# One decoder layer on one core: 1 KB instead of 16 for software DMA descriptors, three more 4 KB slots, 49 expert tiles fetched ahead

## The chip, the cores and the metric

The kernel runs on one core of a Trainium2 chip. The metric is the device time of one launch in microseconds (us); three runs of the kernel before gave 512.88, 513.37 and 514.83 us, and their median, 513.37 us, is what the changed kernel is held against. The engines are named PE (matmul), PEld (its weight load), DVE, ACT, POOL and SP; in this kernel every load and store is issued by SP.

## The reference, cut to what matters

The layer takes x of shape 256 x 1024 (float32). Four token mixers run side by side, are gated, summed and projected, and the result is normalised. The second half is a mixture of experts, and the tiles that the change fetches sooner belong to it:

```
lg, le = x @ wr_g, x @ wr_e            # router: group, then two experts of its eight
h  = silu(x @ w_gate[e]) * (x @ w_up[e]) * gate[e]
y += h @ w_down[e]                     # for each of 32 experts
x  = layer_norm(alpha * x + y)
```

`w_gate` and `w_up` are 1024 x 256 for each expert, `w_down` 256 x 1024: 3 MB for each expert, 96 MB for all 32, each read once.

## The kernel before, in words

**Slots.** Most working tiles of 4 KB on each of the 128 partitions (512 KB in all) come from a pool `rp` of `NW` = 35 slots: weights as they arrive (`w`), the halves that a weight is split into (`hi`, `lo`), activations and masks. `slot` takes one. A slot is given to a new tile only when the readers and writers of the tile that held it are done; whatever writes the new tile first (a DMA, ACT, DVE or POOL) waits for that. A second pool, `rb`, with `NR` = 13 slots, is opened when the token mixers have ended (`gen_X`), in the SBUF that they leave.

**Order.** The first half is a set of generators, one letter each, and the string `ORDER` says which of them takes its next step. The program's order on every engine is the order in which the steps are written down. `S` splits projection weights and loads the next ones (line 246), `P` multiplies, `A` to `D` are the mixers, `U` and `O` the output projection, `Q`, `R`, `Y`, `Z` and `E` the router, the normalisation (`nrm`, line 1417, which reads `xtok`) and the gather of the first group of experts. `L` is one step of `gen_L`, which calls `fetch`.

**Expert tiles.** The experts run in eight groups (`NQUAD`) of four. For a group come eight tiles of `mwg` (gate), eight of `mwu` (up) and eight of `mwd` (down), 512 KB each: 192 tiles in a fixed list, `stream`; the `mwd` tiles of the last two groups stand at its end. `fetch` takes the next tile of the list, gives it a slot, from `rb` or `rp` by its number (`RB <= n % (NR + NF) < RB + NR`, with `NF` = 33, so 46 slots in turn), and issues its DMA on SP (line 1235). `gen_L` fetches the first `NL` = 46 within `ORDER`; from then on each tile is fetched in `wload`, where its group begins to use tiles and none is left in the list of fetched ones. The last eight tiles are loaded in halves (line 1242).

**A group** is: gate and up products (line 1527, PE, four experts side by side), the transposes of the scatter matrix (1477), the gather for the next group (1429), silu and product (1547 to 1549), a transpose (1552), the down product (1496) and the scatter into the accumulated result (1514; 1642 for the last group). Behind the last group come the statistics (1649, 1661), the scaling (1610, 1614, POOL's 1669) and the stores (1615, 1677).

The DMAs are numbered over eight semaphores, DMAHW0 to DMAHW7 in turn, and each DMA's issue waits for the landing of the one eight before it; so eight are under way at most.

Of the kernel before, what the change touches and what calls it, by code (L numbers as in the profile page):

```python
# [113 lines left out]
def _layout(inp):  # L114
# [81 lines left out]
MID = 8  # L196
NEAR = 6

NW = 35
NR = 13  # L200
NF = 33
N2 = 19
N1 = 10
NL = 46
RB = 0
LATE = 2
WARM = 5
# [7 lines left out]
    "ADDSAAADDAAABAAAABADDDDBDDDBBDDBBPDBBSDBSBBBBBBDDPDDBBBPCBCBPCSBBCBASPCLCMMCCCCCDMNCMCMCPCCSCCNCPSCP"  # L215
    "PSCPMMNPSPSMPCNMMMCCCDMNPPMSMPSMPSNPMCXLLMLLLLLLLPSPSPSPMPSPPSLPNNMLLMLLLSPMSLMLPSPLPSMPSPMNNPMLPSPS"
    "MMMPSMPSMNNMMMLMMPLMPSPSUMMPMMPMUUSUMUPMMUMPMMMPOUOLMLLLLMLULLUOULLLULMOUULULLMOUUOUUOQOQLQQQQQQQQLQ"
    "QYYLQQUQQQQORLOLLLRLRQRRLRQRRQRRRRQRRRZQZQERRRRRRRLRREQEEQRRE"
)


def body(ctx, tc, I, out):
# [6 lines left out]
    cp = ctx.enter_context(tc.tile_pool(name="cp", bufs=1))  # L229
    rp = ctx.enter_context(tc.tile_pool(name="rp", bufs=NW))  # L230

# [7 lines left out]
    def slot(name, shape, pool=None, dt=F32):  # L239

        t = (pool or rp).tile([P, 1024], dt, tag="w", name=name)
        return view(t, int(np.prod(shape[1:])), shape)
# [986 lines left out]
    def fetch():  # L1229
        n = len(fetched)  # L1230
        src, (e, k), shape = stream[n]
        t = slot("w", shape, MP["rb"] if RB <= n % (NR + NF) < RB + NR else rp)
        fetched.append(t)
        if n < len(stream) - 8:
            SY.dma_start(t, I[src][e][k])
            return

        tails.append((t, I[src][e][k]))
        if n == len(stream) - 1:
            for hs in (slice(0, 512), slice(512, 1024)):  # L1240
                for t, a in tails:
                    SY.dma_start(t[:, hs], a[:, hs])

    def gen_L():
        yield "X"
        for i in range(NL):
            fetch()
            if i + 1 < NL:
                yield 0
# [498 lines left out]
```

## Time and profile before

| | |
|---|---|
| median of three runs | 513.37 us (512.88 to 514.83) |
| the profiled execution | 511.94 us, of which the span of its instructions 510.2 us |
| PE busy | 467.2 us, 92% of the span |
| PEld busy | 357.0 us, 70% |
| DVE / ACT / POOL busy | 241.7 / 195.8 / 47.0 us |
| bytes moved | 146.82 MB, 288 GB/s over the span |
| granted TensorE clock, mean | 0.981 |

The span holds two programs in a row: up to 300 us the mixers, the projection and the router, from 300 us on the eight groups of experts. Shares over the whole span are means of the two. In windows of 20 us and of the end the DMA engines are less than half busy between 60 and 200 us, and from 308 us until the loads end they are busy all the time.

### The profile page before, as it was taken

The page shows a single profiled execution, that of the slowest core. Times are in us where ns is not written, and L with a number is a line of the kernel's source. Part 1 is how long each engine was busy: PE and PEld are TensorE (multiplying, and loading weights), DVE is VectorE, ACT ScalarE, POOL GpSimd, SP SyncE. Part 2 cuts the span into 40 slices and gives each one's busy share as a digit, 9 for nine tenths or more (in the row PEclk, how much of TensorE's full clock was granted, in tenths as well). Part 3 has the DMA queues.
Part 4 walks back from the last instruction along what each step waited for, and adds up shares of the span by engine and source line. Part 5 has one row for each costly group of instructions (what it writes and reads, how often), then busy time and mean ns, then how long its engine had stood idle before and what let it go on. Part 6 is the DMA issues. An engine that isn't in the chain of part 4 may idle for free. (4 is left out here: it accounts for less than half of the span.)

```text
span 510.2 us, 10633 instructions
## 1 busy us (share of the span) xinstructions
PE 467.2 (92%) x4396; PEld 357.0 (70%) x4396; DVE 241.7 (47%) x479; ACT 195.8 (38%) x357; POOL 47.0 (9%) x55
## 2 busy tenths in 40 slices
PE   8999999999999999999999899998898989777891
PEld 6888887998778999999998676554453635343420
DVE  4786659987868558544764643021111211111015
ACT  5967555366494465434353342020201201001311
POOL 2003022300000012123150000000000000000002
PEclk9999999999999999999999989999999999989896
DMA  8999432212332452999879869999999999999962
GB/s 283 350 371 383 141 110 84 89 39 84 123 127 84 145 187 90 408 410 409 336 288 413 287 242 406 407 409 408 409 408 408 409 409 409 408 410 408 401 239 84
DMA packets 44410, 146.82 MB, mean 288 GB/s; under 512 B 4996, under 2 KB 7624, under 8 KB 44360
## 3 DMA queue, kind: packets, MB, share of 16 engines
q1 hardware_dynamic: 44360, 146.12, 75.0%
q8 instruction: 35, 0.57, 0.4%
q14 instruction: 15, 0.12, 0.1%
HBM read 143.48 MB, written 2.62 MB: 286 GB/s over the span
## 5 line engine op out<-in xcount | busy, mean ns | idle before, releaser
L374 PE MATMUL ps<-xl,hi 128*128 128x256 f32 x416 | 122.3, 294 | 1.9 <-DVE vS L385 1.1
L375 PE MATMUL ps<-xh,lo 128*128 128x256 f32 x416 | 118.0, 284 | 0.4 <-DVE lo L360 0.3
L376 PE MATMUL ps<-xh,hi 128*128 128x256 f32 x416 | 117.6, 283 | 0.0
L360 DVE TENSOR_TENSOR lo<-w,hi 128x1024 fp32r<-128x1024 f32 (+1 forms) x75 | 89.1, 1206 | 53.1 <-ACT hi L359 45.5
L374 PEld LDWEIGHTS ps<-xl,hi 128*128 128x128 f32 x416 | 79.7, 192 | 5.6 <-issue 1.9
L375 PEld LDWEIGHTS ps<-xh,lo 128*128 128x128 f32 x416 | 79.7, 192 | 2.6 <-issue 1.4
L359 ACT CAST hi<-w 128x1024 fp32r<-128x1024 f32 (+1 forms) x75 | 74.2, 1014 | 16.9 <-PE ps L375 5.1
L376 PEld LDWEIGHTS ps<-xh,hi 128*128 128x128 f32 x416 | 79.7, 192 | 0.0
L1527 PE MATMUL ps<-w,xg 128*32 128x256 f32 x1024 | 69.0, 393 | 7.8 <-DMA w<-mwu 7.0
L1527 PEld LDWEIGHTS ps<-w,xg 128*32 128x32 f32 x1024 | 34.0, 112 | 39.7 <-DMA w<-mwu 12.2
L1429 PE MATMUL ps<-Sel,nrm 128*128 128x128 f32 x256 | 33.6, 286 | 1.3 <-DVE smr L1395 0.7
L1429 PEld LDWEIGHTS ps<-Sel,nrm 128*128 128x128 f32 x256 | 31.3, 200 | 4.8 <-issue 4.1
L1514 PE MATMUL ps<-small,SGT 128*128 128x512 f32 x48 | 23.7, 616 | 9.1 <-DVE small L1508 5.1
L1508 DVE COPY small<-ps 128x512 f32<-128x512 f32 x6 | 4.2, 692 | 53.2 <-PE ps L1514 53.2
L1479 ACT COPY SGT<-ps 128x256 f32<-128x256 f32 x8 | 3.0, 373 | 65.8 <-PE ps L1477 65.8
L1496 PE MATMUL ps<-w,small 128*32 128x512 f32 x192 | 24.7, 599 | 3.7 <-ACT xg L1436 3.0
L1514 PEld LDWEIGHTS ps<-small,SGT 128*128 128x128 f32 x48 | 8.2, 189 | 24.9 <-DVE small L1508 10.1
L1669 POOL TENSOR_TENSOR res<-res,ln 128x512 f32<-128x512 f32 x1 | 1.7, 1730 | 239.2 <-ACT res L1668 239.2
L1422 DVE TENSOR_TENSOR Sel<-rank,csts 128x128 f32<-128x128 f32 x16 | 4.0, 288 | 32.7 <-PE ps L1477 32.7
L374 PE MATMUL ps<-parts,hi 128*128 128x256 f32 x64 | 18.8, 293 | 0.0
L1496 PEld LDWEIGHTS ps<-w,small 128*32 128x32 f32 x192 | 5.4, 109 | 18.3 <-ACT xg L1436 7.5
L375 PE MATMUL ps<-parts,lo 128*128 128x256 f32 x64 | 18.1, 283 | 0.0
(417 smaller groups left out, 703.2 us busy)
## 6 DMA issues: line engine op xcount, KB each, us to landing
w<-mwg SPq DMA_DIRECT2D x64, 512.0 KB, 10.2
w<-mwu SPq DMA_DIRECT2D x64, 512.0 KB, 10.2
w<-mwd SPq DMA_DIRECT2D x56, 512.0 KB, 10.2
w<-win SPq DMA_DIRECT2D x54, 512.0 KB, 5.4
w<-wbr SPq DMA_DIRECT2D x8, 512.0 KB, 4.1
w<-wout SPq DMA_DIRECT2D x8, 512.0 KB, 7.9
w<-mwd SPq DMA_DIRECT2D x16, 256.0 KB, 5.3
scr<-fsb SPq DMA_DIRECT2D x1, 1536.0 KB, 7.0
```

Source lines behind the costliest of these rows:

```text
L359: A.copy(hi, src)
L360: V.tensor_tensor(lo, src, hi.bitcast(F32), op=OP.subtract)
L374: T.matmul(dst, lhsT=ls[0], rhs=rs[1], start=start, stop=False)
L375: T.matmul(dst, lhsT=ls[1], rhs=rs[0], start=False, stop=False)
L376: T.matmul(dst, lhsT=ls[0], rhs=rs[0], start=False, stop=stop)
L1422: V.tensor_tensor(t, rank[q][:, 4 * g:4 * g + 4, None].broadcast_to([P, 4, 32]), C("iota")[:, None, :].broadcast_to([P, 4, 32]), op=OP.is_ ...
L1429: T.matmul(pg[:, k4], lhsT=nrm[q][:, 128 * k:128 * k + 128], rhs=f2(SelR[g, q]), start=q == 0 and k4 == 0, stop=True, skip_group_check=True)
L1479: A.copy(SGT, pg)
L1496: T.matmul(pd[h][32 * e4:32 * e4 + 32], lhsT=outs[g][0][:, k, 32 * e4:32 * e4 + 32], rhs=wds[g][k][e4][:, 512 * h:512 * h + 512], start=k ...
L1508: V.tensor_copy(dn[h], pd[h])
L1514: T.matmul(yacc[q, h], lhsT=outs[g][1][:, q], rhs=dn[h], start=False, stop=False, skip_group_check=True)
L1527: T.matmul(pgu[32 * e4:32 * e4 + 32, i], lhsT=xg[:, k, 32 * e4:32 * e4 + 32], rhs=ws[k // 4][e4][:, k % 4, :], start=k == 0, stop=k == KT ...
```

## The change

[...] 

```
-NW = 35
+NW = 38
 NR = 13
-NF = 33
+NF = 36
-NL = 46
+NL = 49
@@ the last row of ORDER
-    "QYYLQQUQQQQORLOLLLRLRQRRLRQRRQRRRRQRRRZQZQERRRRRRRLRREQEEQRRE"
+    "QYYLQQUQQQQORLOLLLRLRQRRLRQRRQRRRRQRRRZQZQERRRRRRRLRREQEEQRRELLL"
@@ def kernel
-    nc = _bacc.Bacc("TRN2", target_bir_lowering=False, num_devices=1)
+    nc = _bacc.Bacc("TRN2", target_bir_lowering=False, num_devices=1, dynamic_dma_scratch_size=1024)
```

No engine gets an instruction more or less, and none stands in another place in its engine's order. What differs is which slot a tile takes, and so what the first writer of a tile waits for. On SP, around the end of `ORDER`, the fetches stand as follows; the number behind `w_` counts the program's tiles, and a name in brackets is a semaphore: DMAHW0 to 7 of the DMA eight before, PE, Activation, DVE and Pool of the readers and writers of the tile that held the slot. Before:

```order
L1235 DMA w_3609<-mwd 128x1024 [waits DMAHW2_49,PE_49]
L1235 DMA w_3675<-mwd 128x1024 [waits DMAHW3_49,Activation_49]
L1235 DMA w_4012<-mwd 128x1024 [waits DMAHW4_49,PE_49]
L1235 DMA w_4014<-mwd 128x1024 [waits DMAHW5_49,PE_49]
L1235 DMA w_4054<-mwg 128x1024 [waits DMAHW6_49,PE_49]
L1235 DMA w_4056<-mwg 128x1024 [waits DMAHW7_49,PE_49]
L1235 DMA w_4058<-mwg 128x1024 [waits DMAHW0_49,PE_49]
```

And now:

```order
L1235 DMA w_3609<-mwd 128x1024 [waits DMAHW2_49,PE_49]
L1235 DMA w_3675<-mwd 128x1024 [waits DMAHW3_49,PE_49]
L1235 DMA w_3721<-mwd 128x1024 [waits DMAHW4_49]
L1235 DMA w_3723<-mwd 128x1024 [waits DVE_49,PE_49,DMAHW5_49,Activation_49,Pool_49]
L1235 DMA w_3725<-mwg 128x1024 [waits DMAHW6_49,Activation_49]
L1235 DMA w_4056<-mwg 128x1024 [waits DMAHW7_49,PE_49]
L1235 DMA w_4058<-mwg 128x1024 [waits DMAHW0_49,PE_49]
```

`w_3675` is the 46th fetch in both. Before, the 47th, 48th and 49th (`w_4012`, `w_4014`, `w_4054`) are written down in groups 1 and 2 of the experts and take the slots of the first, second and third fetched tile, which PE reads at line 1527 of group 0. Now (`w_3721`, `w_3723`, `w_3725`) they take slots of `rp` in which a tile of the router or the normalisation lay, and the 50th, `w_4056`, is the first to wait for PE's reading of the first fetched tile.

On POOL, at 44 us in the span, the clearing of `qx` (a tile of mixer C) takes another slot. Before:

```order
L667 TENSOR_TENSOR Cm<-LB,cst 128x256 [waits DVE_49]
L1027 MEMSET qx 128x1024 [waits Pool_49]
L686 TENSOR_TENSOR Cm<-LB,cst 128x256
L686 TENSOR_TENSOR Cm<-LB,cst 128x256 [waits PE_49,Activation_49]
L686 TENSOR_TENSOR Cm<-LB,cst 128x256 [waits PE_49,Pool_49]
```

And now:

```order
L667 TENSOR_TENSOR Cm<-LB,cst 128x256 [waits DVE_49]
L1027 MEMSET qx 128x1024 [waits DMAHW4_49,DVE_49]
L686 TENSOR_TENSOR Cm<-LB,cst 128x256
L686 TENSOR_TENSOR Cm<-LB,cst 128x256 [waits PE_49]
L686 TENSOR_TENSOR Cm<-LB,cst 128x256 [waits PE_49,Pool_49]
```

The slot is now one in which a weight lay that DVE reads at line 360 to make its `lo`; `Cm` (mixer D's triangular blocks) stand behind it on POOL.

## Rows read from the trace of the kernel before

**Rows 1.** Windows: stretch, length, PE, PEld, DVE, ACT, POOL busy, PEclk, DMA share, GB/s.
```profile
0.00:284.00 284.00, 278.13 (x2624) 253.30 (x2624) 191.64 (x324) 156.67 (x265) 43.97 (x53) 1.00 0.62 227
...
284.00:287.00 3.00, 2.76 (x17) 2.32 (x16) 1.35 (x7) 2.06 (x4) 0.00 (x0) 1.00 0.35 85
287.00:299.00 12.00, 10.05 (x65) 8.82 (x64) 6.56 (x29) 4.80 (x11) 0.00 (x0) 0.86 0.94 342
299.00:302.00 3.00, 3.00 (x54) 1.94 (x56) 2.14 (x12) 2.17 (x8) 0.00 (x0) 1.00 0.04 14
302.00:305.00 3.00, 3.00 (x54) 1.58 (x50) 1.25 (x6) 0.37 (x1) 0.00 (x0) 1.00 0.72 205
...
308.00:494.00 186.00, 163.06 (x1541) 86.03 (x1540) 30.01 (x87) 27.43 (x64) 0.00 (x0) 0.98 1.02 404
494.00:495.00 1.00, 1.00 (x3) 0.19 (x1) 0.65 (x1) 0.00 (x0) 0.00 (x0) 1.00 0.02 6
```

**Rows 2.** SP's waits, 312 to 500 us: total us, times, longest.
```profile
SPq L1235 <- DMA w<-mwu: 41.9, 47, 1.3
...
SPq L1235 <- PE ps L1527: 7.5, 10, 4.8
```

**Rows 3.** DMA: queue with packets, MB, share; issues with count, size, us to landing.
```profile
q1 hardware_dynamic: 44360, 146.12, 75.0%
...
w<-mwu SPq DMA_DIRECT2D x64, 512.0 KB, 10.2
```

**Rows 4.** PE's waits, 437 to 458 us (the group of experts before the last).
```profile
PE ps L1527 <- DMA w<-mwu: 3.7, 5, 1.1
...
PE ps L1527 <- DMA w<-mwg: 0.5, 1, 0.5
```

**Rows 5.** PE's waits, 458 to 500 us (the last group and the end).
```profile
PE ps L1527 <- DMA w<-mwu: 3.3, 5, 0.7
...
PE ps L1527 <- DMA w<-mwg: 0.4, 1, 0.4
```

**Rows 6.** Timeline of PE, 405 to 512 us; in brackets its wait and for what.
```profile
416.25 3.66 PE L1527 MATMUL ps<-w,xg 128*32 128x256 f32 x64
...
453.05 3.47 PE L1527 MATMUL ps<-w,xg 128*32 128x256 f32 x26 [0.66 <-DMA w<-mwu]
...
463.27 1.91 PE L1527 MATMUL ps<-w,xg 128*32 128x256 f32 x26 [0.40 <-DMA w<-mwg]
...
473.58 3.52 PE L1527 MATMUL ps<-w,xg 128*32 128x256 f32 x26 [0.66 <-DMA w<-mwu]
...
495.10 1.06 PE L1496 MATMUL ps<-w,hh 128*32 128x512 f32 x8
```

**Rows 7.** Windows at the granted clock's two low stretches, and in the end.
```profile
453.30:456.60 3.30, 3.30 (x27) 1.38 (x19) 0.00 (x0) 0.04 (x1) 0.00 (x0) 0.50 1.03 411
473.80:477.10 3.30, 3.29 (x26) 1.22 (x18) 0.00 (x0) 0.00 (x0) 0.00 (x0) 0.50 1.03 410
478.60:497.00 18.40, 17.62 (x111) 7.89 (x111) 2.09 (x3) 6.05 (x10) 0.00 (x0) 1.00 0.80 295
```

**Rows 8.** SP's waits, 255 to 312 us.
```profile
SPq L1235 <- PE ps L1527: 7.9, 2, 7.0
...
SPq L1235 <- ACT nrm L1417: 4.4, 1, 4.4
```

**Rows 9.** Timelines of ACT and PE near 300 us: start, length, what.
```profile
292.94 1.24 ACT L1417 ACTIVATE nrm<-xtok,nmr,mv 128x1024 f32<-128x1024 f32 x1 [1.34 <-DVE rank L1389]
...
299.53 3.66 PE L1527 MATMUL ps<-w,xg 128*32 128x256 f32 x64
```

**Rows 10.** Timelines of POOL and DVE near 44 us.
```profile
44.50 0.95 POOL L1027 MEMSET qx<- 128x1024 f32 x1
45.41 1.43 POOL L686 TENSOR_TENSOR Cm<-LB,cst 128x256 f32<-128x256 f32 x2
...
48.13 2.36 DVE L360 TENSOR_TENSOR lo<-w,hi 128x1024 fp32r<-128x1024 f32 x2 [4.00 <-ACT hi L359]
```

**Rows 11.** Tile Cm: its reader on PE (ns min/median/max, first to last start).
```profile
L635 PE MATMUL ps<-XY,Cm x160: 218/218/267, 62.2 to 109.4; 64*64 64x64 f32 x160
```

## The prediction

> **What bounds the kernel now.** I read windows first, because a share over the whole span mixes two programs. Up to 284 us PE is busy 278.13 of 284 us while the DMA engines are at 0.62 [rows 1]: PE is the bound there, and no fetch that comes sooner helps it. From 308 to 494 us the DMA share is 1.02 at 404 GB/s [rows 1]; in that stretch SP's own waits are for the DMA eight places before (41.9 us in 47 waits for the `mwu` tiles alone), and its waits for a slot, 7.5 us on PE's line 1527, are at most 4.8 us long [rows 2]. A tile lands 10.2 us after its issue with eight under way [rows 3], so a stall of 4.8 us on SP still leaves the engines tiles to move. From 308 us on the loads are thus one unbroken stream, and the last packets of it go at 494 us: the share falls to 0.02 in the next microsecond [rows 1].
>
> Does the end hang on that stream? PE's waits say where. PE lives on the stock of tiles fetched ahead; in the last two groups the stock is gone. It waits for tiles 3.7 + 0.5 = 4.2 us in the group before the last [rows 4] and 3.3 + 0.4 = 3.7 us in the last [rows 5], 7.9 us in all. The last `mwu` tile starts PE's final 26 products at 473.58, behind a wait of 0.66 us for it [rows 6]; what follows to the end of the span at 510.2 is PE's work at 17.62 of 18.40 us and then DVE's. And PE's last eight down products stand at 495.10 [rows 6], 1.1 us behind the last packets. So the end follows the stream, with 1.1 us of play at most.
>
> The third thing is when the stream starts. Between 299 and 302 us the DMA engines stand at 0.04 [rows 1]: SP waited 7.0 us in one piece for PE's line 1527 [rows 8], that is, for group 0 to free the slot of the first fetched tile, and its products begin at 299.53 [rows 9].
>
> **The change part by part.** Before, the fetches 47 to 49 are the ones that stand in this hole. In the order now, the 47th waits for nothing but the DMA before it, the 49th for Activation, and the 48th for all four engines, none of them at work in the experts yet. What ACT ends last among the tiles of `rp` is `nrm`, which reads `xtok`: 292.94 + 1.24 = 294.18 us [rows 9]. That is the release on which the 46th fetch stood before, for 4.4 us [rows 8]; now it is the 49th's. So all three are issued by about 294.5 us, some 7 us before PE frees the first expert tile.
>
> Is there room for them? Idle time of the DMA engines: 0.65 of 3 us from 284, 0.06 of 12 us from 287, 0.96 of 3 us from 299 [rows 1], or 2.0 + 0.7 + 2.9 = 5.6 us. A tile costs 10.2 / 8 = 1.28 us of the engines, three 3.8 us. They fit, and none of them delays the 50th, which now takes the place of the 47th behind the same PE instructions, with the same slow first microseconds (0.72 from 302 to 305 us [rows 1]). From there every tile lands when the one three places before it did: **3.8 us sooner**, to the last packets at 490.2. A slot's release behaves alike: each later fetch waits for the tile 49 before instead of 46, and lies three places further on.
>
> What PE makes of it: the final `mwu` tile comes at 469.8 instead of 473.58. Without any wait PE would stand there 7.9 us sooner, at 465.7; so it still waits for that tile and takes the 3.8 us in full, with 7.9 - 3.8 = 4.1 us of waits left. They vanish first where they come first: in the group before the last 4.2 - 3.8 = 0.4 us should be left, and all 3.7 in the last. From the last `mwu` tile on nothing is changed, and all of it moves by 3.8 us.
>
> [...]
>
> The granted clock is the term with two ends. [...] With 0.4 us of waits left in the group before the last I expect its low stretch to go; that brings PE 1.6 us nearer to tiles that have not landed, and turns into waiting in the last group (3.7 + 1.6 = 5.3 us). If the second one goes as well, PE could gain 1.6 us more behind the last `mwu` tile, but no more than the 1.1 us before it meets the last packets. If one falls into the 18.40 us that now run at 1.00 [rows 7], it costs 1.6 us. I take zero, as the pattern of tiles in the last group stays, and keep -1.1 and +1.6.
>
> Cost at nothing, with the cover named. Slots in the first 284 us: loads and ACT's and DVE's splits get theirs sooner or when they did; PE's 278.13 us hide it. POOL is the exception: the clearing of `qx`, done from 44.50, now waits for DVE's line 360, whose pair runs from 48.13 to 50.49 [rows 10], so up to 6.0 us; two `Cm` of 1.43 us stand behind it on POOL. They would end at about 52.9, and PE reads its first `Cm` at 62.2 [rows 11]: 9 us of cover. Without it the 6 us would go into mixer D's chain. The smaller descriptor space: the loads and stores go through the hardware queue, 44360 packets [rows 3], so nothing here writes descriptors by software. New addresses for tiles: the 64 gate products of a group take 3.66 us in group 0 [rows 9] and 3.66 in group 5 [rows 6], from other slots, so I take nothing on either side.
>
> Sum: the profiled execution took 511.94 us, 510.2 in the span and 1.7 around it. It becomes 506.4 + 1.7 = 508.1. The three timed runs lie 0.9 to 2.9 us above it, the median by 1.4; I carry that over: **509.5 us**.
>
> **Rivals.** (a) The three are not early. If a slot stayed held to group 0, as that of the 47th was (7.0 us [rows 8]), the stream starts as before: 513.4. The order speaks against it, the 47th's only wait being a DMA; for it, that the 48th waits for all four engines, and SP is in order, so one late release there holds everything behind it. (b) A low stretch of the clock moves into the end: 509.5 + 1.6 = 511.1. Rows 7 show that it falls after bursts with waits between, and the last group will have more of these.
>
> (c) Slower: the clock stays low through the end. PE, sooner at the last group, waits longer; where the low grant then lasts from 469.8 over the PE work of 17.62 us [rows 7], that takes up to 17.62 x 1.6 / 1.91 = 14.8 us more, 524 us. Half of it gives 517. It decides from 3.8 us of loss, or three low stretches in the end instead of none. Against it: both low stretches here ended while PE was in dense work, and 478.60 to 497 ran at 1.00. [...] (d) PE, not the stream, leads the end: no waits, 509.5 - 1.1 = 508.4 at best, being held by the last packets.
>
> **How the numbers follow.** The forecast has 0.72, (a) 0.10, (b) 0.09, (c) 0.04, (d) 0.05. About 0.5% (2.6 us) is what a measurement here can tell from no change, so the border is 510.8. Runs of one kernel spread by 2 us, so a median of three may lie 0.7 off: the forecast and (d) fall above the border about one time in twelve, (b) below it two in five. Faster 0.72 x 0.92 + 0.05 + 0.09 x 0.4 = 0.75; same 0.20, from (a), most of (b) and the strays; slower 0.05. The range goes from (d) less 0.6, 507.8, to (b) with 1.1 more, 512.2; it leaves out (a) and (c), and strays, under 0.2.
>
> **What would show it.** Right: no DMA hole of 3 us with a 7 us stall of SP on line 1527 behind the 46th fetch, but three tiles more landed before it; last packets near 490; PE's waits for tiles near 4 to 6 us, nearly all in the last group; span near 506. Wrong: a stall of SP on the 47th or 48th fetch into 299 us; last packets at 490 while the end stays (then the end does not hang on the stream); last packets at 494. Granted clock under 1.00 between 475 and 493 would be (b) or (c).

## The result

The changed kernel took 508.51 us (median of 7 runs, 508.08 to 511.98), the kernel before, run beside it, 514.72 (7 runs, 512.46 to 517.45): ratio 0.990, 95% interval 0.9865 to 0.9935. Measured again later it took 510.78 us (11 runs) against 512.71 (14 runs): 0.9938, interval 0.9899 to 0.9978. The ratios here and below are those on record with their intervals, not the quotients of the medians, which would be 0.988 and 0.996. By the two ratios the gain is 0.6 to 1.0%, 3 to 5 us, and the forecast of 509.5 us lies between the two medians. One run each of before (512.91 us below is the median of the other 24), of the kernel with three fetches fewer and of the one with the delay at group 0 was in a slower state and is left out of ratios and medians.

The profiled execution of the changed kernel, however, took 511.98 us with a span of 510.2, as long as the one of before (511.94 and 510.2), where 508.1 was forecast. The windows of the changed kernel, columns as in [rows 1], say where that comes from:

```profile
0.00:284.00 284.00, 277.99 (x2612) 253.74 (x2612) 191.88 (x322) 155.49 (x263) 44.11 (x53) 0.99 0.62 228
284.00:287.00 3.00, 2.51 (x20) 2.22 (x19) 1.89 (x6) 1.36 (x5) 0.00 (x0) 0.93 1.03 412
287.00:299.00 12.00, 10.70 (x54) 8.98 (x55) 6.71 (x29) 5.25 (x8) 0.00 (x0) 0.78 0.88 315
299.00:302.00 3.00, 2.31 (x16) 2.22 (x15) 0.60 (x4) 0.79 (x4) 0.00 (x0) 0.79 0.70 277
302.00:305.00 3.00, 3.00 (x47) 2.19 (x49) 2.08 (x10) 1.77 (x7) 0.00 (x0) 1.00 0.00 0
308.00:490.00 182.00, 159.38 (x1571) 86.54 (x1564) 30.35 (x87) 27.18 (x64) 0.00 (x0) 0.98 1.02 404
491.00:494.00 3.00, 3.00 (x26) 1.09 (x19) 0.00 (x0) 0.58 (x1) 0.00 (x0) 1.00 0.74 270
494.00:495.00 1.00, 1.00 (x3) 0.19 (x1) 0.60 (x1) 0.00 (x0) 0.00 (x0) 1.00 0.01 4
```

The stream runs at 1.02 and 404 GB/s as before, and its last packets go at 494 us as before. But the hole ahead of it now lies at 302 to 305 us, 3 us later than in [rows 1], and the granted clock was 0.78 ahead of it instead of 0.86. PE's timeline shows what that did, first of before (two rows ahead of the one in [rows 9]):

```profile
293.30 3.44 PE L1429 MATMUL ps<-Sel,nrm 128*128 128x128 f32 x16 [0.58 <-DVE Sel L1422]
297.57 2.02 PE L1429 MATMUL ps<-Sel,nrm 128*128 128x128 f32 x16 [0.70 <-DVE smr L1395]
```

and of the changed kernel:

```profile
296.65 3.65 PE L1429 MATMUL ps<-Sel,nrm 128*128 128x128 f32 x16 [0.59 <-DVE Sel L1422]
301.17 2.02 PE L1429 MATMUL ps<-Sel,nrm 128*128 128x128 f32 x16 [0.69 <-DVE smr L1395]
303.12 3.66 PE L1527 MATMUL ps<-w,xg 128*32 128x256 f32 x64
```

PE comes to group 0's first product at 303.12 us, where it came at 299.53. One gather ran at a granted clock of 0.50 in both executions (3.44 and 3.65 us for what takes 2.02); the changed kernel's had two more low stretches ahead of that, of 3.4 us at 0.50 each, at 10.1 us in the first projection tile and at 286.6 in the last products of the projections. Counted from group 0's first product, the end of the span came 510.2 - 299.53 = 210.7 us later in the kernel before, and 510.2 - 303.12 = 207.1 us now: 3.6 us less.

SP's waits, 255 to 312 us, answer to [rows 8]:

```profile
SPq L1235 <- PE ps L1527: 9.3, 3, 7.3
...
SPq L1235 <- ACT nrm L1417: 1.4, 1, 1.4
```

SP still stands 7.3 us on line 1527: but with three more tiles issued. The first `mwg` tile in SP's timeline from 285 to 312 us is the 49th fetch in both kernels; before, and then in the changed one:

```profile
303.24 4.88 SPq L1235 DMA_DIRECT2D w<-mwg  x8
```

```profile
297.53 12.62 SPq L1235 DMA_DIRECT2D w<-mwg  x8
```

It was issued 3.7 us behind group 0's first product before, and goes 5.6 us ahead of it now. PE's waits for tiles, 437 to 460 and then 460 to 512 us, answer to [rows 4, 5]:

```profile
PE ps L1527 <- DMA w<-mwu: 3.3, 5, 0.7
```

```profile
PE ps L1527 <- DMA w<-mwu: 2.6, 4, 0.7
PE ps L1527 <- DMA w<-mwg: 1.8, 2, 1.1
```

### The profile page after: what moved, and what is told of

It reads as the page before. It is cut to its first block, busy times and chain, and to the rows that moved or that the text cites. A ratio compares the mean times of both kernels' runs of the same rounds, so it can differ in the third digit from the quotient of the medians.

```text
span 510.2 us, 10618 instructions
## 1 busy us (share of the span) xinstructions
PE 467.1 (92%) x4396; PEld 359.7 (71%) x4396; DVE 243.5 (48%) x479; ACT 195.1 (38%) x357; POOL 47.0 (9%) x55
## 2 busy tenths in 40 slices
DMA packets 44410, 146.82 MB, mean 288 GB/s; under 512 B 4996, under 2 KB 7624, under 8 KB 44360
## 3 DMA queue, kind: packets, MB, share of 16 engines
q1 hardware_dynamic: 44360, 146.12, 74.9%
## 5 line engine op out<-in xcount | busy, mean ns | idle before, releaser
L360 DVE TENSOR_TENSOR lo<-w,hi 128x1024 fp32r<-128x1024 f32 (+1 forms) x75 | 90.5, 1228 | 44.8 <-ACT hi L359 44.6
L1527 PE MATMUL ps<-w,xg 128*32 128x256 f32 x1024 | 67.8, 393 | 7.7 <-DMA w<-mwu 5.9
L1527 PEld LDWEIGHTS ps<-w,xg 128*32 128x32 f32 x1024 | 33.8, 112 | 38.6 <-DMA w<-mwu 10.2
L1496 PE MATMUL ps<-w,small 128*32 128x512 f32 x192 | 23.1, 598 | 3.5 <-ACT xg L1436 3.0
L1514 PEld LDWEIGHTS ps<-small,SGT 128*128 128x128 f32 x48 | 8.2, 189 | 25.0 <-DVE small L1508 10.1
L374 PE MATMUL ps<-parts,hi 128*128 128x256 f32 x64 | 18.8, 294 | 0.0
L376 PE MATMUL ps<-parts,hi 128*128 128x256 f32 x64 | 18.1, 283 | 0.0
## 6 DMA issues: line engine op xcount, KB each, us to landing
w<-mwg SPq DMA_DIRECT2D x64, 512.0 KB, 10.1
w<-mwu SPq DMA_DIRECT2D x64, 512.0 KB, 10.2
w<-mwd SPq DMA_DIRECT2D x56, 512.0 KB, 10.2
w<-win SPq DMA_DIRECT2D x54, 512.0 KB, 7.0
w<-wbr SPq DMA_DIRECT2D x8, 512.0 KB, 3.4
w<-wout SPq DMA_DIRECT2D x8, 512.0 KB, 9.0
```

What stands on the lines that cost most here:

```text
L360: V.tensor_tensor(lo, src, hi.bitcast(F32), op=OP.subtract)
L374: T.matmul(dst, lhsT=ls[0], rhs=rs[1], start=start, stop=False)
L376: T.matmul(dst, lhsT=ls[0], rhs=rs[0], start=False, stop=stop)
L1496: T.matmul(pd[h][32 * e4:32 * e4 + 32], lhsT=outs[g][0][:, k, 32 * e4:32 * e4 + 32], rhs=wds[g][k][e4][:, 512 * h:512 * h + 512], start=k ...
L1514: T.matmul(yacc[q, h], lhsT=outs[g][1][:, q], rhs=dn[h], start=False, stop=False, skip_group_check=True)
L1527: T.matmul(pgu[32 * e4:32 * e4 + 32, i], lhsT=xg[:, k, 32 * e4:32 * e4 + 32], rhs=ws[k // 4][e4][:, k % 4, :], start=k == 0, stop=k == KT ...
```

## The experiments

The ruler for all of them is one distance: from group 0's first product to PE's last eight down products, which start 0.3 to 0.5 us behind the landing of the last expert tile in both kernels. From there to the end of the span it is 15.0 to 15.1 us in each of the executions below. What the clock did ahead of group 0 drops out of that distance; what it does behind does not. Before it is 495.10 - 299.53 = 195.57 us [rows 6, 9]; in the changed kernel 192.03, by this row of its timeline:

```profile
495.15 1.06 PE L1496 MATMUL ps<-w,hh 128*32 128x512 f32 x8
```

**The descriptor space alone.** The kernel before with

```
+ num_devices=1, dynamic_dma_scratch_size=1024
```

> The kernel before with the 1 KB descriptor space alone, still 35 slots and 46 fetches ahead. Theory (the gain is three tiles more in the hole before group 0): no change, ratio 1.00 within 0.5%, and 210.7 us from group 0's first product on line 1527 to the end of the span, as before (510.2 - 299.53). Rival (the smaller descriptor space itself, or the addresses that it moves, gives some of the gain): a ratio near 0.99.

Measured: 512.30 us against 512.91 beside it, ratio 0.9985 (0.9962 to 1.0008). Its timeline of PE:

```profile
301.15 3.80 PE L1527 MATMUL ps<-w,xg 128*32 128x256 f32 x64
...
496.50 1.06 PE L1496 MATMUL ps<-w,hh 128*32 128x512 f32 x8
```

The distance is 195.35 us, that of before within 0.2. The descriptor space gives nothing by itself.

**The slots without the fetches.** The changed kernel with

```
-NF = 36
+NF = 33
-NL = 49
+NL = 46
```

and without the three `L` at the end of `ORDER`.

> The changed kernel with its three further slots, but 46 fetches ahead, so that the slots serve the first part alone. Theory: group 0's first product to the end of the span takes 210.7 us as before, ratio 1.00; the 47th fetch waits again for PE's line 1527, some 7 us. Rival (freer slots in the first 284 us bring PE to group 0 sooner): the first product stands at 295 to 298 us with the clock at 1.00, and the ratio is near 0.99.

Measured: 513.55 us against 512.91, ratio 0.9988 (0.9957 to 1.002). SP's waits, 255 to 312 us, and PE's timeline:

```profile
SPq L1235 <- PE ps L1527: 13.7, 4, 11.3
```

```profile
301.66 3.66 PE L1527 MATMUL ps<-w,xg 128*32 128x256 f32 x64
...
496.96 1.07 PE L1496 MATMUL ps<-w,hh 128*32 128x512 f32 x8
```

The distance is 195.30 us. Slots that are only free sooner make SP wait longer for PE (11.3 us in one piece, not the 7 that I expected) and change no end: in the first 284 us PE is busy for 278.13 [rows 1].

**Three fewer.** The kernel before with

```
-NF = 33
+NF = 30
-NL = 46
+NL = 43
```

> The kernel before with three fetches ahead fewer, 43 instead of 46. Theory (each tile that isn't in before group 0 comes behind the others at 1.28 us): 210.7 + 3.8 = 214.5 us from group 0's first product to the end, ratio about 1.007, PE's waits for tiles in the last two groups about 3.8 us longer. Rival (PE, not the stream, sets the end, and the gain came from elsewhere): 210.7 us, ratio 1.00.

Measured: 517.61 us (5 runs) against 512.91, ratio 1.0108 (1.0073 to 1.0143). SP's waits and PE's timeline:

```profile
SPq L1235 <- PE ps L1527: 16.6, 5, 14.6
```

```profile
300.68 3.81 PE L1527 MATMUL ps<-w,xg 128*32 128x256 f32 x64
...
500.65 1.07 PE L1496 MATMUL ps<-w,hh 128*32 128x512 f32 x8
```

199.97 us: 4.4 to 4.7 more than with 46, where 3.8 were expected. The direction is the theory's, and PE's waits for expert tiles at line 1527 (420 to 505 us) were 8.9 + 2.6 = 11.5 us against 7.9 before, 3.6 us longer, as expected. Why a tile is worth 1.5 us here and 1.2 between 46 and 49 isn't settled (the engines are dry for longer here, SP's one wait being 14.6 us).

**One more.** The changed kernel with

```
-NW = 38
+NW = 39
-NF = 36
+NF = 37
-NL = 49
+NL = 50
-dynamic_dma_scratch_size=1024
+dynamic_dma_scratch_size=256
```

and a fourth `L`.

> The changed kernel with one slot more (39) and 50 fetches ahead, its descriptor space cut to 256 bytes for it. Theory: another 1.28 us sooner, 207.1 - 1.3 = 205.8 us from group 0's first product to the end, about 5.0 us less than before, ratio 0.990. Rival (after three the hole is full or PE leads the end): 207.1 us, as the changed kernel.

Measured: 508.47 us against 512.91, ratio 0.9924 (0.9898 to 0.995); span 506.4.

```profile
301.15 3.66 PE L1527 MATMUL ps<-w,xg 128*32 128x256 f32 x64
...
491.39 1.06 PE L1496 MATMUL ps<-w,hh 128*32 128x512 f32 x8
```

190.24 us, 1.8 less than with 49 (1.6 less than in the repetition below). By the distance the fiftieth tile still pays; the ratio can't tell it from the changed kernel's.

**PE held up ahead of group 0, and ahead of group 3.** The changed kernel with four products into a bank that nothing reads, `g == 0` in one kernel, `g == 3` in the other:

```
 xg = XG.pop(g)
+if g == 0:
+    pw = ps([P, 512], pj)
+    for _ in range(4):
+        T.matmul(pw, lhsT=ident, rhs=nrm[0][:, 0:512], start=True, stop=True)
```

> The changed kernel with PE held up at the start of group 0: four products of 128x512 into a bank that nothing reads, some 3.6 us of PE by the 64 products of line 1527 (256 columns, 3.66 us for 16 passes). Theory (the stream restarts when group 0's products free the first expert tile, so what delays PE before them delays the end one for one): 207.0 + 3.6 = 210.6 us from the last gather product of line 1429 before group 0 to the end, ratio to before near 1.00; SP's stall on PE's line 1527 some 3.6 us longer. Rival (the stream goes on by itself and PE has play): 207 us, ratio 0.99.

> The changed kernel with the same four products at the start of group 3 instead of group 0. Theory (from 308 us the stream sets the end, PE has waits for tiles of 7.7 us in the last two groups to give): no loss, 207.0 us from the gather to the end, PE's waits for tiles in the last two groups 3.6 us shorter, 4.1 us. Rival (PE is the bound of the last 200 us): 210.6 us.

Measured, on one chip: 513.24 us (9 runs) with the delay at group 0 and 509.74 us (10 runs) with it at group 3, 3.5 us apart; ratios to before 1.0038 (1.0001 to 1.0074) and 0.993 (0.9902 to 0.9957). PE's timeline with the delay at group 0:

```profile
297.42 2.02 PE L1429 MATMUL ps<-Sel,nrm 128*128 128x128 f32 x16 [0.70 <-DVE smr L1395]
299.28 3.60 PE L1523 MATMUL ps<-nrm,csts 128*128 128x512 f32 x8
302.81 3.66 PE L1531 MATMUL ps<-w,xg 128*32 128x256 f32 x64
...
494.10 1.07 PE L1496 MATMUL ps<-w,hh 128*32 128x512 f32 x8
```

and at group 3:

```profile
297.92 3.66 PE L1531 MATMUL ps<-w,xg 128*32 128x256 f32 x64
...
489.59 1.06 PE L1496 MATMUL ps<-w,hh 128*32 128x512 f32 x8
```

From the end of the last gather (299.44 us) to the end of the span it is 509.1 - 299.44 = 209.7 us with the delay at group 0, where the changed kernel has 510.2 - 303.19 = 207.0: 2.7 of the 3.4 us by which the first product was held up came out at the end in this execution, 3.5 in the medians. SP's wait on the gate products grew from 7.3 to 10.4 us. With the same work at group 3 the distance is 191.67 us, not longer than without it: PE's waits for tiles took it up. These were 4.6 + 1.3 = 5.9 us instead of 5.9 + 1.8 = 7.7 (420 to 505 us), not the 4.1 that I expected; here no low stretch lay ahead of PE's last wait for a tile (it came at 468 us, with that wait), where the changed kernel had one (1.6 us, at 464 us), and PE waits what it gains by that.

**PE kept at work in its gaps.** To the kernels with 50 fetches (the first of two) and with 49 (the second) products are added that nothing reads, where PE stands idle ahead of group 0. In both, the added products go with `start=True` into PSUM banks that also hold sums of the router (in the first also a tile of the first projection), and I take it that these sums lose terms by that: the outputs are off by a relative 0.23 and 0.12. All instructions of the reference are there.

```
+T.matmul(bank[:, 128:256], lhsT=ident, rhs=ident, start=True, ...)   # ahead of four router products
+keep(3)   # three such, into the bank of the ranks, ahead of each gather of group 0
+T.matmul(pair[:, 1], lhsT=h[:, k], rhs=xp(k)[0], ...)   # x5, first kernel alone: first projection tile, k == 1 and 3
```

> The kernel with 39 slots and 50 fetches ahead, and in it PE does products that nothing reads where it stands idle: five behind each of the second and fourth k of the first projection tile, one ahead of each of the four groups of router products, three ahead of each gather of group 0. [...] Rival (the low stretches come whatever PE does there, or the end does not follow): 506.4 us of span or more, ratio 0.992.

> The changed kernel (38 slots, 49 fetches) with the router's and the gather's idle gaps filled in the same way, and nothing at the start. Theory: no low stretch between 280 us and group 0, group 0's first product 1.6 to 3.3 us sooner than the 303.12 us of the changed kernel, 207.1 us from it to the end, runs near 508 us without the group at 511. Rival: as the changed kernel, with runs at 508 and at 511.

Measured: the first 506.96 us against 513.39, ratio 0.9864 (0.9836 to 0.9891); the second 508.71, ratio 0.9912 (0.988 to 0.9943). For the first I had expected no low stretch between 280 us and group 0 and some 504 us of span. It had one all the same, in the gather, and its span was 508.1:

```profile
293.34 0.91 PE L1319 MATMUL ps<-csts 128*128 128x128 f32 x6
294.86 3.68 PE L1442 MATMUL ps<-Sel,nrm 128*128 128x128 f32 x16 [0.61 <-DVE Sel L1435]
```

The row before it says what I did wrong: the three products took 0.91 us, and the wait of 0.61 us for DVE still came behind them. The gather starts 1.74 us behind the second rank product (293.12 us), where it starts 0.97 us behind it without the added products (292.18 and 293.15 us with the delay at group 0). DVE reads the ranks in the same bank, and I take it that it waited for the added products; the next kernels, with another bank, bear that out. They moved the gap instead of filling it. In the second there was no low stretch ahead of 500 us, but group 0's first product stood at 299.84 us, no sooner than before.

**The same, mended.** The added products write to banks that no engine reads at that time, two instead of three ahead of each gather, and four behind the second `k` of the first projection tile; the one ahead of each four router products stays, with `start` set only where the sum begins. With 50 fetches and 39 slots. The second kernel leaves out the four at the start, the third is the changed kernel again.

```
+T.matmul(pg[1][:, 0], lhsT=ident, rhs=ident, ...)           # x2, ahead of the gather's first half
+T.matmul(banks[0][:, 128:256], lhsT=ident, rhs=ident, ...)  # x2, behind the second rank product
+T.matmul(pw, lhsT=h[:, k], rhs=xp(k)[0], ...)               # x4, first projection tile, k == 1
```

> The kernel with 39 slots and 50 fetches ahead, with products that nothing reads in PE's idle gaps, fewer and better placed than in the earlier kernel of this kind: four behind the second k of the first projection tile, one ahead of each group of router products, two ahead of each gather of group 0 in banks that no other engine reads then. It computes the whole reference. Theory (PE reaches group 0 at full clock and unhindered, and the end follows it): group 0's first product at 297.5 to 298.5 us, the last expert tile some 190 us behind it, the end 15.4 us behind that, 503 to 504 us of span, ratio to before 0.982 to 0.986. Rival (the low stretch comes all the same, or the added products cost what they save): 506 us of span, ratio 0.992 as with one slot more alone.

> The same without the four products in the first projection tile. Theory: as the one with them where the first projection runs at full clock, and some 2 us later in the executions in which it falls low there; median 0.5 to 1.5 us above it. Rival (the gap at the start doesn't matter): the same median.

> The changed kernel once more, unedited, on the chip of the two others. Theory: group 0's first product to the last expert tile 191.6 us, and to the end 207.1 us, wherever the low stretches fall; ratio to before 0.990. Rival (the 207.1 was one execution's luck): a distance 1 us or more off.

Measured, on one chip: 506.74 us (5 runs, 506.06 to 507.65), ratio 0.9848 (0.9794 to 0.9902); without the four at the start 507.44 (505.75 to 507.97), 0.9854 (0.980 to 0.9907); the changed kernel 510.78 (508.27 to 514.42), 0.9938. PE's timeline of the first:

```profile
293.02 0.69 PE L1456 MATMUL ps<-csts 128*128 128x128 f32 x4
293.77 2.05 PE L1439 MATMUL ps<-Sel,nrm 128*128 128x128 f32 x16
295.66 0.31 PE L1389 MATMUL ps<-oh,csts 128*128 128x32 f32 x2
295.80 0.69 PE L1394 MATMUL ps<-csts 128*128 128x128 f32 x4
296.66 2.02 PE L1439 MATMUL ps<-Sel,nrm 128*128 128x128 f32 x16 [0.17 <-DVE smr L1405]
298.62 3.66 PE L1538 MATMUL ps<-w,xg 128*32 128x256 f32 x64
...
489.30 1.06 PE L1507 MATMUL ps<-w,hh 128*32 128x512 f32 x8
```

Both gathers take 2.0 us, the wait of 0.6 us is gone and that of 0.7 is 0.17, and the granted clock is 1.00 from 6 us in the span to 497. Group 0's first product, at 298.62 us, is 0.1 us behind the 297.5 to 298.5 that I expected. The distance is 190.68 us (190.57 in the second), as with 50 tiles before. Whether the four at the start are worth anything stays open: 0.7 us between the medians, with ranges that overlap. What filling the gaps is worth stays open in part as well: against the kernel with 50 fetches and its gaps left (508.47 us, measured on another chip) it is 1.0 to 1.7 us by the medians, and the intervals of the ratios overlap at their ends. The mean granted clock was 0.993 and 0.994 in the two profiled executions and 0.982 to 0.989 in the other eight runs, so these had more low stretches; where they lay isn't on record.

The changed kernel's second profile is the other extreme:

```profile
297.41 3.09 PE L1429 MATMUL ps<-Sel,nrm 128*128 128x128 f32 x16 [0.59 <-DVE Sel L1422]
301.46 3.72 PE L1429 MATMUL ps<-Sel,nrm 128*128 128x128 f32 x16 [0.69 <-DVE smr L1395]
305.12 3.66 PE L1527 MATMUL ps<-w,xg 128*32 128x256 f32 x64
...
496.98 1.07 PE L1496 MATMUL ps<-w,hh 128*32 128x512 f32 x8
```

Both gathers were low, and two stretches ahead of them; its span is 512.0 us, and the distance 191.86.

All in one table. The low time is the sum of the stretches, of 3.4 us each, in which the granted clock was 0.50, from 7 us in the span to group 0's first product:

| execution | fetched ahead | us at a clock of 0.50 ahead of group 0 | first product | distance | span |
|---|---|---|---|---|---|
| three fewer | 43 | 6.8 | 300.68 | 199.97 | 515.7 |
| before | 46 | 3.4 | 299.53 | 195.57 | 510.2 |
| descriptor space alone | 46 | 6.8 | 301.15 | 195.35 | 511.6 |
| slots without fetches | 46 | 6.8 | 301.66 | 195.30 | 512.0 |
| changed | 49 | 10.2 | 303.12 | 192.03 | 510.2 |
| changed, again | 49 | 17.1 | 305.12 | 191.86 | 512.0 |
| delay at group 0 | 49 | 3.4 | 302.81 | 191.29 | 509.1 |
| delay at group 3 | 49 | 0 | 297.92 | 191.67 | 504.6 |
| gaps filled, second kernel | 49 | 0 | 299.84 | 191.68 | 506.6 |
| one more | 50 | 6.8 | 301.15 | 190.24 | 506.4 |
| gaps filled, first kernel | 50 | 3.4 | 302.00 | 191.10 | 508.1 |
| gaps filled, mended | 50 | 0 | 298.62 | 190.68 | 504.4 |
| without the start | 50 | 0 | 298.37 | 190.57 | 504.0 |

The distance goes by the number of tiles: 195.3 to 195.6 us with 46, 191.3 to 192.0 with 49, 190.2 to 191.1 with 50. Where no product was added, the first product goes by the clock, 0.4 to 0.55 us later for each us at 0.50, and the span is the sum of the two and 15.

The 191.10 us, the longest with 50, has its own cause. The first kernel with added products and the one with one more tile come to the same down products at the same time behind the same wait; in the first the granted clock was 0.50 from 475.9 to 479.2 us, in the other 1.00:

```profile
475.69 3.48 PE L1510 MATMUL ps<-w,hh 128*32 128x512 f32 x10 [0.23 <-DMA w<-mwd]
```

```profile
475.63 1.90 PE L1496 MATMUL ps<-w,hh 128*32 128x512 f32 x10 [0.23 <-DMA w<-mwd]
```

From there to the last eight down products PE took 17.41 us instead of 15.76.

## Why the prediction was right, point by point

**What bounds the kernel: right.** The loads are one stream at 1.02 from 308 us, the end follows its last tiles, and the stream starts with group 0's first products. A delay of PE at group 0 came out at the end, and the same delay at group 3 did not. The prediction allowed 1.1 us of play at the end; there is less, since the last eight down products read the last tile and start 0.3 us behind its landing in the execution before. PE shows no wait for that tile; its last wait for one is 0.66 us for the last `mwu` tile [rows 6], and what it lost behind that is 0.5 us at most, worked out below.

**Three tiles, 3.8 us: right, slightly too much.** The distance went from 195.3 to 195.6 down to 191.7 to 192.0, 3.3 to 3.9 us. The three were issued ahead of group 0, the 49th at 297.53 us instead of the 294.5 that I forecast, behind `nrm`, which came later with PE. The fourth in the hole was worth another 1.0 to 1.8 us.

**The profiled execution, 508.1 us: wrong, 511.98.** The step that failed is "the 50th ... behind the same PE instructions": the same ones, but 3.6 us later. I took PE's arrival at group 0 as a given, because nothing of the change touches it, and put a clock term only behind it. The trace of before had the warning in [rows 1], a mean of 0.86 between 287 and 299 us. So the sign "no DMA hole of 3 us" wasn't met either: the hole was there, at 302 to 305 us, with no packet in it. The term that I left out is larger than the whole gain: 297.92 us without a low stretch, 305.12 with the most seen.

Whether the change has a part in the low stretches isn't shown. The three executions with 46 fetches had 3.4 to 6.8 us of them, the changed kernel 10.2 and 17.1, and with the delays 3.4 and 0. The difference is the low stretch in the first projection tile and a second one from 286.6 to 288.0 us on: the changed kernel's two executions and the one with slots but no fetches have both, the other ten neither. In these three PE waited 1.36 to 1.71 us in one piece in that first tile, in the others at most 1.01 us. All three have 38 slots, but so have three of the ten. The mean granted clock over all runs shows no clear difference: 0.983 and 0.981 in the two series of the changed kernel, 0.982 to 0.983 in those of before.

The forecast of the median held all the same: in effect it is the median of before less 3.8 us, and the profiled execution of before cancels out of it. The one of the changed kernel was the longest of its seven runs, and four of them took 508.1 to 508.5 us.

**The waits of PE: wrong in size.** 7.9 - 3.8 = 4.1 us were to be left, and 7.7 were measured. One part is in the 7.9, which is too small. Where PE's groups start shows it, before

```profile
432.21 1.90 PE L1496 MATMUL ps<-w,small 128*32 128x512 f32 x10 [0.23 <-DMA w<-mwd]
...
439.59 2.36 PE L1527 MATMUL ps<-w,xg 128*32 128x256 f32 x38
```

and in the changed kernel

```profile
441.37 3.66 PE L1527 MATMUL ps<-w,xg 128*32 128x256 f32 x64
...
474.11 3.45 PE L1527 MATMUL ps<-w,xg 128*32 128x256 f32 x26 [0.66 <-DMA w<-mwu]
```

Before, the group that starts at 416.25 us [rows 6] takes 23.34 us to the next one at 439.59; its like in the changed kernel starts at 419.84 and takes 21.53. So the stock of tiles had run out one group sooner, and 1.8 us were lost there of which the waits show 0.23. I had read PE's waits in the last two groups and not the period of the groups. The kernels with the descriptor space alone and with slots but no fetches, 46 tiles both, took 23.9 us there as well. From the next group's start to the last `mwu` tile's products it is 473.58 - 439.59 = 33.99 us before and 474.11 - 441.37 = 32.74 in the changed kernel, 1.25 us less, while the waits in it fell by 0.2 alone: the profile counts 26.1 us of busy PE in the first stretch and 25.0 in the second for the same products, so part of what PE lost there shows as busy time. The last 0.5 us came behind the last `mwu` tile, where I had expected nothing (495.10 - 473.58 = 21.52 us, now 495.15 - 474.11 = 21.04): 24 down products took 3.20 us before and 2.78 now. These three parts, 1.8 + 1.25 + 0.5, make up the distance's 3.5 us.

**The clock's low stretches near the end: half right.** The prediction's 1.6 us for a low stretch are the 3.47 and 3.52 us that 26 products took in the two at 0.50 [rows 7], less the 1.91 of 26 others [rows 6]. The first stretch, at 453 us, went: the 26 products at 453.18 took 1.92 us. But another came at 464 us, in the last group. Windows of the two in the changed kernel, which answer to [rows 7]:

```profile
464.10:467.50 3.40, 3.40 (x27) 1.42 (x20) 0.00 (x0) 0.00 (x0) 0.00 (x0) 0.50 1.03 410
474.40:477.70 3.30, 3.16 (x26) 1.19 (x18) 0.00 (x0) 0.10 (x1) 0.00 (x0) 0.50 1.03 412
```

That the first of these cost nothing agrees with "I take zero": PE waits for the next tiles either way. The second cost 0.2 us at most: from the last `mwu` tile's products to the last eight down products the changed kernel took 21.04 us, the one with one more tile, at 1.00 there, 491.39 - 470.51 = 20.88. No low stretch reached beyond 479.2 us in any profile of 46 or 49 tiles until the kernel's last 10 us, so (b) and (c) did not come in these. The sign that I named for them, a clock under 1.00 between 475 and 493 us, was a bad one: it was met to 477.7 us, but before it is met as well [rows 7].

**Costs at nothing: right.** `qx` was cleared at 51.11 us and the two `Cm` behind it ended at 53.5, where 52.9 was estimated, ten microseconds ahead of PE's first read at 63.9. The slots without the fetches gave 0.9988, the descriptor space alone 0.9985.

**The rivals.** (a) fell: the 47th to 49th were issued ahead of SP's stall. (b) was seen once, in the first kernel with added products, whose low stretch from 475.9 us on cost PE 1.65 us, close to the 1.6 of the prediction; its last eight down products started 1.9 us behind the last landing, and its distance was 0.4 to 0.9 us longer than the others' with 50 tiles. (d), PE in the lead without waits, was not seen: 7.7 us of waits were left.

Both mended kernels, with the gaps ahead of group 0 filled, show a granted clock of 1.00 there. The gaps were 0.2 to 0.7 us each around the router and the gathers, and at most 1.7 us in the first projection tile, and with them left as they are one profile of the changed kernel's program (with the delay at group 3) shows 1.00 as well. That filling the gaps is what kept the clock up is thus likely, not shown.

## What to carry to other kernels

Where a stream of loads is the bound and starts only when an engine frees the first buffer, time that engine's arrival and the stream's length apart. Here each tile that was in before the start was worth 1.0 to 1.8 us by the distance, where the estimate was 1.28. A delay of PE ahead of the start came out at the end for the most part (2.7 of 3.4 us in one trace), behind it not at all while PE had waits for tiles left (a distance of 191.67 us with the delay at group 3, 191.86 and 192.03 without). The smaller descriptor space gave nothing by itself (0.9985); the three tiles that the slots in it let come sooner took 3.3 to 3.9 us off the distance. And when one profile of a 1% change disagrees with the medians, look for a distance inside the trace that the disturbance doesn't touch.

## What the runs showed of the hardware

- The granted clock of one program differs from run to run: ahead of group 0 the changed kernel spent 10.2 us at a clock of 0.50 in one profile and 17.1 in another, and its runs went from 508.08 to 514.42 us. With 50 tiles they went from 507.31 to 510.63 with PE's gaps left and from 505.75 to 507.97 with them filled, on two chips.
- With 0.91 us of products that nothing reads in the bank that DVE reads, the gather behind them started 1.74 us behind the second rank product, 0.8 us later than without them; with 0.69 us of them in a bank that no engine read then it started where it had (0.97 us behind), and PE had no wait.
- With `dynamic_dma_scratch_size` at 256 bytes all 298 loads and stores of the kernel, the 50 fetches among them, ran as before, their 44360 packets on the queue that the profile names hardware_dynamic. How large that space is without the argument, the title's 16 KB, no run shows.
